# Moving S5 outputs and z tiles ahead of the last SSD units, and four weight loads at once

## The chip, the core and the metric

The kernel runs on one core of a Trainium2 chip. The metric is the device time of one launch in microseconds. A core has TensorE (PE in the profile), VectorE (DVE), ScalarE (ACT), GpSimd (POOL) and SyncE (SP), each with an instruction queue of its own that is worked off in order, and 16 DMA engines. Nearly all transfers of this kernel are issued by SP's queue: a transfer whose buffer isn't free holds back the transfers queued behind it.

## What is computed

A block of a bidirectional encoder on x of 2048 tokens by 1024 features, float32. Cut to what matters here:

```
h = rms_norm(x, norm_mix_w)
z, xbc, dt, u = split(h @ w_in)               # 1024 | 2048 | 32 | 512 columns
xbc = silu(dwconv5(xbc));  xs, B, C = split(xbc)
y1 = ssd_scan(forward) + ssd_scan(backward) + d * xs   # 16 heads, 4 groups, chunks of 128 tokens
y1 = rms_norm(y1 * silu(z), ssd_norm_w)
y  = s5_scan(u, forward) + s5_scan(u, backward) + d * u # 32 groups of 16 channels, 64 states
g  = gelu(y);  gl = g @ glu_w + glu_b          # per group, 16 -> 32
y2 = rms_norm(gl[:16] * sigmoid(gl[16:]), s5_norm_w)
x  = x + concat(y1, y2) @ w_out
up = dwconv3(rms_norm(x, norm_ffn_w) @ w_up);  val, gate = split(up)
x  = rms_norm(x + (silu(gate) * val) @ w_down, norm_final_w)
```

## The kernel before

Every float32 product is done as three matmuls of split operands: a high part hi and the rest lo, hi*hi (L444), lo*hi (L445) and hi*lo (L446). A weight or an activation is therefore split first, one cast on ScalarE and one operation on VectorE.

**Stages.** From 0 to 290 us the input is transposed (pt, L500), normalised and multiplied with u's columns of w_in (pu). Until 705 us the second half of the tokens is worked off, and beside it the S5 recursion, mainly on GpSimd. From 705 us the first half of the tokens: the four SSD groups, z tiles, and S5 outputs between them. From about 1187 us the out projection (the matmuls named p), then from 1560 us the FFN as Strassen products.

**A group** (L804) makes four conv tiles (each a projection of 128 columns over 1024 tokens, pmm, and its convolution on VectorE) and then eight SSD units, one for each chunk of 128 tokens. A **unit** (L742) loads decay rows (rw, L747), takes exponentials (L764), multiplies masks and scores (L766, L767), runs small matmuls (ptb L756 and L757, pyd L770 and L776, pst L791), puts together yy (L778, L779, L781), stores it to y_d (L783), and carries the state in sb (L790, L801, L802). A **z tile** (L698) projects 128 columns over 1024 tokens and stores them to z_d. **S5 outputs** (L369) of one index b are four groups of matmuls s5py (L386), Gelu to s5gt (L394), matmuls s5pgl (L400), a tanh (L403) and two operations to s5vl (L405, L406), stored to ys_d (L407).

**out_weights** (L813) splits w_out in twelve pieces (raw loads woraw into a pool of six buffers that the group's four conv tiles share; casts L824, splits L825). **out_pre** (L827) reads the results back: ztt from z_d (L832), yt from y_d (L834), ysT from ys_d (L867); yt times ztt (L851), a cast (L439), and the out matmuls.

**u_weights** (L535) loads u's columns of w_in in four pieces of 512 KB (L543) through two raw buffers (wraw) and splits each into wu.

**What sets the order.** Instructions are put on their engines by a scheduler that simulates a timeline, with the priority of the program's order. Tables at the head say where work is written: OC[g] holds the indices of the S5 outputs written ahead of group g (OC[4] behind group 3), ZC[g] the z tiles ahead of group g of the first half.

Of the kernel before, what the change touches and what calls it, by code (L numbers as in the profile page):

```python
# [21 lines left out]
S5W = 512  # L22
# [6 lines left out]
ZA = 4  # L29
GA = 4  # L30
ZB = ((4,), (5,), (6,), (7,))
OC = ((), (0, 1), (2, 3), (4, 5), (6, 7))
ZC = ((), (0,), (1, 2), (3,), (4, 5, 6, 7))


def bcast(ap, axis, n):
# [380 lines left out]
class Block:  # L417
# [114 lines left out]
            nc.scalar.activation(hi, pt, AF.Copy, scale=w)  # L532
            nc.vector.scalar_tensor_tensor(lo, pt, w, hi.bitcast(F32), ALU.mult, ALU.subtract)

    def u_weights(self, sp, wp):  # L535
        nc = self.nc
        wv = self.A["w_in"][0].rearrange("(k p) n -> p k n", p=P)
        self.wu = [sp.tile([P, 8, S5W], F32R, name=f"wu{j}") for j in range(2)]
        raw = lambda c: wp.tile([P, 8, P], F32, name="wraw", tag="wraw", bufs=2).rearrange("p k n -> p (k n)").rearrange(
            "p (k n) -> p k n", n=c)  # L540
        for k in range(0, 8, 2):
            r = raw(S5W)
            nc.sync.dma_start(r, wv[:, k:k + 2, W_U:W_U + S5W])  # L543
            self.split(self.wu[0][:, k:k + 2], self.wu[1][:, k:k + 2], r)
        self.wd = sp.tile([P, 8, 64], F32R, name="wd")
        r = raw(32)[:, 0:8]
        nc.sync.dma_start(r, wv[:, :, W_DT:W_DT + 32])
        self.split(self.wd[:, :, 0:32], self.wd[:, :, 32:64], r)
        self.us = [sp.tile([P, 2, 8, 64], F32, name=f"us{m}") for m in range(4)]
# [251 lines left out]
                v.tensor_tensor(S, S, bcast(self.decb[:, ch, 16 + 4 * g:16 + 4 * g + 4], 2, 64), ALU.mult)  # L801
                v.tensor_tensor(self.sb[:, g], self.sb[:, g], st[:, 256:512], ALU.add)  # L802

    def group(self, mp, wp, sp, ps, pp, ht, half, g):  # L804
        cols = [(8 + g, W_B + 128 * g), (12 + g, W_C + 128 * g),
                (2 * g, W_X + 256 * g), (2 * g + 1, W_X + 256 * g + 128)]
        sl = [self.conv_tile(mp, wp, ps, ht, half, mt, c0) for mt, c0 in cols]
        self.nc.sync.dma_start(self.ct_d[g][:, 1024 * half:1024 * half + 1024], sl[1])
        for c in range(7, -1, -1):
            self.ssd_unit(sp, pp, g, 8 * half + c, sl)  # L810
# [387 lines left out]
def hybrid_block_kernel(ctx: ExitStack, tc: tile.TileContext, *aps):  # L1198
    nc = tc.nc
    A = dict(zip(_INS, aps[:-1]))  # L1200
    b = Block(nc, tc, A, aps[-1])
# [6 lines left out]
    with ExitStack() as mix:  # L1208
# [14 lines left out]
        ht = b.new_ht(hp)  # L1223
# [3 lines left out]
        with pool(name="s0", bufs=1) as sp, right("s5cs") as cs:  # L1227
            with right("s5prm") as sr:
                b.norm_block(sp, wp, pp, ht, 0, 2)
                b.u_weights(sp, wp)  # L1230
                p0 = tc.cur_priority
                soon = lambda: tc.high_priority(offset=tc.cur_priority - p0)
                b.u_dt(sp, ps, ht, 0, 2)
                with soon():
                    b.norm_block(sp, wp, pp, ht, 1, 514)
                b.u_dt(sp, ps, ht, 1, 514)
                with soon():
                    for i in range(2):
                        nc.scalar.copy(ht[i][:, :, 0:2], ht[i][:, :, 1024:1026].bitcast(F32))
                for j in (2, 3):  # L1240
                    with soon():
                        b.norm_block(sp, wp, pp, ht, j, 512 * j - 1022)
                    b.u_dt(sp, ps, ht, j, 512 * j - 1022)
                with soon():
                    s5.params(cs, sr)
                    b.main_consts(mk, sr, s5.pst)
            with right("s5tab") as wk:
                with soon():
                    for k in range(NK5):
                        s5.tables(wk, k)  # L1250
                for m in range(ZA):
                    b.z_tile(wp, ps, ht, 1, m)
# [27 lines left out]
        with right("s5o") as so:  # L1280
            s5.out_setup(so)
            for g in range(4):
                for m in ZC[g]:
                    b.z_tile(wp, ps, ht, 0, m)
                for o in OC[g]:
                    s5.outputs(so, o)
                b.group(mp, wp, sp, ps, pp, ht, 0, g)
            for m in ZC[4]:
                b.z_tile(wp, ps, ht, 0, m)
            for o in OC[4]:  # L1290
                s5.outputs(so, o)
        lw.close()
        psg.close()
        wo = ExitStack()
# [2 lines left out]
        nc.vector.tensor_copy(decf, b.decb[:, :, 0:16])  # L1297
        b.decb = decf
        b.fst = wc.tile([P, 4, 256], F32, name="fst")
        b.nfw = b.col(mc, A["norm_ffn_w"][0], 8, "nfw")  # L1300
        b.out_weights(wc, mp)
        psb, psc = ExitStack(), ExitStack()
        ps = psb.enter_context(pool(name="psb", bufs=4, space=PSUM))
# [2 lines left out]
        pth = en(pool(name="pth", bufs=1, space=PSUM, side="right"))  # L1306
        pp = psc.enter_context(pool(name="ppb", bufs=1, space=PSUM, side="right"))
        gp = en(tc.tile_pool(name="gp", bufs=1, side="right", reuse_waits="tile"))
        with right("b1") as sp:
            pre = b.out_pre(sp, gp, ps, pp, 0)  # L1310
            h2 = None
            for ch in range(16):
                cur = pre
                if ch < 15:
                    pre = b.out_pre(sp, gp, ps, pp, ch + 1)
                else:
                    b.ffn_consts(mc, gp, ps)
                last, h2 = h2, b.out_gemm(sp, gp, ps, pp, ch, *cur)
                if ch:
                    b.out_tail(gp, pth, ch - 1, last)  # L1320
                if 10 <= ch < 14:
                    b.tok_sums(gp, 0, ch - 10)
# [48 lines left out]
```

## Time and profile before

| | us |
|---|---|
| median of three runs | 2923.3 |
| lowest and highest run | 2913.18, 2929.7 |
| the profiled execution, its time | 2930.28 |
| its span | 2928.5 |
| TensorE busy | 2701.5 (92%) |
| VectorE busy | 2197.4 (75%) |
| ScalarE busy | 1364.4 (47%) |
| GpSimd busy | 653.9 (22%) |
| mean granted TensorE clock | 0.968 |

The rows are read as follows. A busy share over the whole span mixes stages, so the windows by stage come first. In a timeline each line is one instruction, or a few alike, with its start, its duration, and in brackets how long the engine had stood idle before it and what it then waited for. Durations of instructions that follow each other closely overlap a little. A clock of 1.00 is 2.4 GHz, 0.50 is 1.2 GHz.

### The profile page before, as it was taken

To read this page: it belongs to the slowest core of one execution; us is meant where nothing else is said; L and a number is where in the kernel's file an instruction comes from. 1 tells how busy PE (TensorE), PEld (TensorE's weight loads), DVE (VectorE), ACT (ScalarE), POOL (GpSimd) and SP (SyncE) were. 2 spreads that over 40 slices of the span, in tenths; PEclk is the share of its full clock that TensorE was granted. 3 is DMA by queue.
4 is the path that set the end of the run, shared out by engine and by line. 5 is a ranking of instruction groups with operands and counts; after the bars stand their busy time and mean duration, and the time that the engine had idled before them with its cause. 6 is when DMAs were issued, how large, how long until landed. Compare 5 with 4: busy or idle time off the path is not lost.

```text
span 2928.5 us, 37294 instructions
## 1 busy us (share of the span) xinstructions
PE 2701.5 (92%) x12952; PEld 2181.7 (74%) x12952; DVE 2197.4 (75%) x3255; ACT 1364.4 (47%) x2329; POOL 653.9 (22%) x1133
## 2 busy tenths in 40 slices
PE   6998899876999998899898999999999999999997
PEld 4666899765877886677776878787877777877776
DVE  5997688786786776677767777779887888656587
ACT  4542455444567665334235444446444445333254
POOL 0443499992233332111120000000000000000012
PEclk9999999988999999999998999999999999999999
DMA  4546633448455656957845234325444337456464
GB/s 129 173 133 198 168 114 121 112 128 227 134 175 162 188 163 204 252 170 201 252 141 187 79 108 137 107 77 193 149 136 130 121 131 243 160 204 194 150 233 158
DMA packets 507400, 471.55 MB, mean 161 GB/s; under 512 B 90364, under 2 KB 417356, under 8 KB 507212
## 3 DMA queue, kind: packets, MB, share of 16 engines
q1 hardware_dynamic: 504972, 463.99, 52.4%
q0 software_dynamic: 2240, 5.18, 0.7%
q8 instruction: 102, 1.67, 0.2%
q14 instruction: 86, 0.70, 0.1%
HBM read 324.37 MB, written 144.67 MB: 160 GB/s over the span
## 4 chain that ended last, share of the span: by engine, by line
PE 40%; DMA 8%; DVE 7%; issue 2%; ACT 2%; POOL 1%; SPq 0%; ACTq 0%; DVEq 0%; POOLq 0%
PE pA L1040 17%; PE pB L1040 9%; PE pD L1040 5%; PE p L444 3%; PE p L445 2%; PE p L446 2%; DMA ar<-act_d 2%; DVE ll L440 1%; DMA bs<-in_ffn_w_down_dram 1%; DMA wr<-in_ffn_w_up_dram 1%; DMA bs<-hop_d 1%; DMA wt_d<-bs 1%; PE po L846 1%; DVE tl L1027 1%; DMA tst<-in_ffn_w_down_dram 0%
## 5 line engine op out<-in xcount | busy, mean ns | idle before, releaser
L1040 PE MATMUL pA<-th,lh 128*128 128x512 f32 x1056 | 423.7, 402 | 28.3 <-ACT pc L1088 18.8
L1040 PE MATMUL pA<-tl,lh 128*128 128x512 f32 x1056 | 422.1, 400 | 4.2 <-DVE tl L1027 4.2
L1040 PE MATMUL pA<-th,ll 128*128 128x512 f32 x1056 | 420.5, 399 | 0.8 <-DVE ll L440 0.8
L444 PE MATMUL pmm<-hh,wh 128*128 128x512 f32 (+1 forms) x896 | 333.9, 373 | 3.7 <-DVE zt L706 2.4
L445 PE MATMUL pmm<-hl,wh 128*128 128x512 f32 (+1 forms) x896 | 332.7, 371 | 0.0
L446 PE MATMUL pmm<-hh,wl 128*128 128x512 f32 (+1 forms) x896 | 330.2, 369 | 0.0
L1040 PEld LDWEIGHTS pA<-th,lh 128*128 128x128 f32 x1056 | 200.6, 190 | 86.7 <-ACT pc L1088 27.4
L1040 PEld LDWEIGHTS pA<-tl,lh 128*128 128x128 f32 x1056 | 200.7, 190 | 54.2 <-DVE tl L1027 6.4
L1040 PEld LDWEIGHTS pA<-th,ll 128*128 128x128 f32 x1056 | 200.6, 190 | 50.3 <-DVE ll L440 1.6
L1040 PE MATMUL pB<-tl,lh 128*128 128x512 f32 x528 | 209.6, 397 | 1.8 <-DVE tl L1027 1.8
L1040 PE MATMUL pB<-th,lh 128*128 128x512 f32 x528 | 209.7, 397 | 1.8 <-ACT lh L439 1.6
L1040 PE MATMUL pB<-th,ll 128*128 128x512 f32 x528 | 209.2, 397 | 0.0
L1088 ACT COPY pc<-pA 128x512 f32<-128x512 f32 x204 | 116.0, 584 | 185.4 <-PE pA L1040 184.4
L444 PEld LDWEIGHTS pmm<-hh,wh 128*128 128x128 f32 x896 | 169.9, 190 | 30.2 <-issue 3.7
L445 PEld LDWEIGHTS pmm<-hl,wh 128*128 128x128 f32 x896 | 169.8, 190 | 22.6 <-issue 2.5
L764 ACT ACTIVATE Lt<-rw,tokS 128x128 f32<-128x128 f32 x512 | 157.4, 389 | 61.3 <-PE pyd L770 48.7
L446 PEld LDWEIGHTS pmm<-hh,wl 128*128 128x128 f32 x896 | 169.6, 189 | 21.3 <-issue 1.1
L692 DVE SCALAR_TENSOR_TENSOR xbc<-rb,cw,xbc 128x1024 f32<-128x1024 f32 x128 | 178.7, 1399 | 3.8 <-ACT xbc L690 2.8
L444 PE MATMUL p<-wo,yh 128*128 128x512 f32 x384 | 157.3, 410 | 22.2 <-ACT yh L439 21.3
L439 ACT CAST lh<-s 128x512 fp32r<-128x512 f32 (+3 forms) x136 | 109.1, 815 | 123.8 <-DVE s L1007 71.2
L440 DVE TENSOR_TENSOR ll<-s,lh 128x1024 fp32r<-128x1024 f32 (+3 forms) x136 | 126.3, 933 | 52.5 <-PE pA L1040 43.7
L445 PE MATMUL p<-wo,yh 128*128 128x512 f32 x384 | 155.6, 405 | 0.0
(421 smaller groups left out, 6139.0 us busy)
## 6 DMA issues: line engine op xcount, KB each, us to landing
wr<-in_ffn_w_up_dram SPq DMA_DIRECT2D x88, 512.0 KB
rw<-acs_d SPq DMA_DIRECT2D x128, 256.0 KB
wraw<-in_w_in_dram SPq DMA_DIRECT2D x52, 512.0 KB
ar<-act_d SPq DMA_DIRECT2D x32, 512.0 KB
yp_d<-cv SPq DMA_DIRECT2D x32, 512.0 KB
cv<-yp_d SPq DMA_DIRECT2D x32, 512.0 KB
tst<-hop_d SPq DMA_DIRECT2D x28, 512.0 KB
act_d<-cv SPq DMA_DIRECT2D x22, 512.5 KB
```

The lines of the kernel that those rows point to most:

```text
L439: self.nc.scalar.copy(hi, src)
L440: self.nc.vector.tensor_tensor(lo, src, hi.bitcast(F32), ALU.subtract)
L444: mm(ps, lhs[0], rhs[0], start=first, stop=False)
L445: mm(ps, lhs[0], rhs[1], start=False, stop=False)
L446: mm(ps, lhs[1], rhs[0], start=False, stop=last)
L692: nc.vector.scalar_tensor_tensor(ac, rb[:, j:j + 1024], cw(j), ac, ALU.mult, ALU.add)
L764: nc.scalar.activation(Lt[:, d, h], rw[:, d, h], AF.Exp, bias=tk(0, d, h))
L846: nc.tensor.matmul(po[:, 2 * (g - 2 * q) + j], self.fst[:, g, 128 * j:128 * j + 128], ct[:, g], start=True, stop=True)
L1027: nc.vector.tensor_tensor(l, st[:, 0:n], h.bitcast(F32), ALU.subtract)
L1040: mm(ps, x, y, start=first and k == i == 0, stop=k == kt - 1 and i == 2, skip_group_check=not first)
L1088: self.nc.scalar.copy(t, src)
```

## The change

Three edits, all of order and place:

- S5 outputs: three ahead of group 1, three ahead of group 2, two ahead of group 3, none behind it. The last four z tiles are no longer written behind group 3 but between its conv tiles and its units.
- u_weights: the third and fourth raw pieces go into two buffers that S5's tables use later (kt, named rb in the rows), so that no load waits for a buffer.
- The column of norm_ffn_w (nfw, 128x8 elements of 4 bytes) lives in another pool, opened with the out stage.

```
-OC = ((), (0, 1), (2, 3), (4, 5), (6, 7))
-ZC = ((), (0,), (1, 2), (3,), (4, 5, 6, 7))
+OC = ((), (0, 1, 2), (3, 4, 5), (6, 7))
+ZC = ((), (0,), (1, 2), (3,))
...
-            r = raw(S5W)
+            r = raw(S5W) if k < 4 else kt[k // 2 - 2].rearrange("p h g o -> p (h g o)").rearrange("p (k n) -> p k n", n=S5W)
...
-    def group(self, mp, wp, sp, ps, pp, ht, half, g):
+    def group(self, mp, wp, sp, ps, pp, ht, half, g, between=lambda: None):
...
         sl = [self.conv_tile(mp, wp, ps, ht, half, mt, c0) for mt, c0 in cols]
+        between()
...
-                b.u_weights(sp, wp)
+                b.u_weights(sp, wp, s5.kt)
...
                 for o in OC[g]:
                     s5.outputs(so, o)
-                b.group(mp, wp, sp, ps, pp, ht, 0, g)
-            for m in ZC[4]:
-                b.z_tile(wp, ps, ht, 0, m)
-            for o in OC[4]:
-                s5.outputs(so, o)
+                rest = lambda: [b.z_tile(wp, ps, ht, 0, m) for m in range(4, 8)]
+                b.group(mp, wp, sp, ps, pp, ht, 0, g, rest if g == 3 else lambda: None)
...
-        b.nfw = b.col(mc, A["norm_ffn_w"][0], 8, "nfw")
         b.out_weights(wc, mp)
...
+        b.nfw = b.col(gp, A["norm_ffn_w"][0], 8, "nfw")
```

TensorE, from the last z matmul (pmm) on, in the kernel before (s5py and s5pgl are S5 outputs, the others belong to SSD units):

```order
L446 MATMUL pmm<-hh,wl 128x512
L386 MATMUL s5py<-s5uTo,s5tz 128x128
L386 MATMUL s5py<-s5st,s5ot 128x127
L776 MATMUL pyd<-xbc,sb 128x128 x2
L791 MATMUL pst<-xw,xb 128x256
L756 MATMUL ptb<-ident,xbc 128x128 x3
L757 MATMUL ptb<-xbc 128x128
L386 MATMUL s5py<-s5st,s5ot 128x127
L791 MATMUL pst<-xw,xb 128x256
L770 MATMUL pyd<-Lt,xb 64x128 x4
L400 MATMUL s5pgl<-s5gt,s5bd 128x256 x2
```

The same place in the changed kernel:

```order
L446 MATMUL pmm<-hh,wl 128x512
L791 MATMUL pst<-xw,xb 128x256
L757 MATMUL ptb<-xbc 128x128
L756 MATMUL ptb<-ident,xbc 128x128 x3
L757 MATMUL ptb<-xbc 128x128
L791 MATMUL pst<-xw,xb 128x256
L770 MATMUL pyd<-Lt,xb 64x128 x4
L756 MATMUL ptb<-ident,xbc 128x128 x3
L757 MATMUL ptb<-xbc 128x128
L776 MATMUL pyd<-xbc,sb 128x128 x2
L791 MATMUL pst<-xw,xb 128x256
```

Behind the last z matmul stood five units mixed with eight S5 groups; now seven units stand there and nothing else until the out matmuls.

VectorE in the same stretch, before (L825 splits w_out, L405 and L406 are S5's):

```order
L778 TENSOR_TENSOR yy<-eb,pyd 128x256
L801 TENSOR_TENSOR sb<-sb,decb 128x256
L406 SCALAR_TENSOR_TENSOR s5vl<-s5tht,s5vl 128x256
L779 TENSOR_TENSOR yy<-yy,pyd 128x256
L825 SCALAR_TENSOR_TENSOR wo_10989<-woraw,onw,wo_10988 128x1024
L781 SCALAR_TENSOR_TENSOR yy<-xbc,dsk,yy 128x128 x2
L825 SCALAR_TENSOR_TENSOR wo_10989<-woraw,onw,wo_10988 128x1024
L405 TENSOR_SCALAR s5vl<-s5pgl,s5gb 128x256
L802 TENSOR_TENSOR sb<-sb,pst 128x256
```

And in the changed kernel (L826 is the split of w_out):

```order
L802 TENSOR_TENSOR sb<-sb,pst 128x256
L826 SCALAR_TENSOR_TENSOR wo_10985<-woraw,onw,wo_10984 128x1024
L767 TENSOR_TENSOR Lt<-Lt,ptb 128x512
L790 TENSOR_TENSOR xw<-xb,tokS 128x256 x2
L778 TENSOR_TENSOR yy<-eb,pyd 128x256
L801 TENSOR_TENSOR sb<-sb,decb 128x256
L766 TENSOR_TENSOR Lt<-Lt 128x512
L779 TENSOR_TENSOR yy<-yy,pyd 128x256
L826 SCALAR_TENSOR_TENSOR wo_10985<-woraw,onw,wo_10984 128x1024
L781 SCALAR_TENSOR_TENSOR yy<-xbc,dsk,yy 128x128 x2
L802 TENSOR_TENSOR sb<-sb,pst 128x256
```

All twelve splits now stand between the operations of units, and no S5 operation is left there.

SP's queue in the first microseconds, the piece from S5's columns (L228) on (dsk is ssd_d, s5craw the C matrices, wraw raw weights):

```order
 L716 DMA mcr<-in_ssd_conv_w_dram 80x128
+L547 DMA wraw<-in_w_in_dram 128x8x32
 L717 DMA mcr<-in_ssd_conv_b_dram 16x128
-L725 DMA dsk<-in_ssd_d_dram 64x8x1
-L543 DMA wraw<-in_w_in_dram 128x2x512
-L725 DMA dsk<-in_ssd_d_dram 64x8x1
-L424 DMA nfw<-in_norm_ffn_w_dram 128x8x1
-L543 DMA wraw<-in_w_in_dram 128x2x512
+L725 DMA dsk<-in_ssd_d_dram 64x8x1 x2
+L660 DMA wraw<-in_w_in_dram 128x8x128
 L219 DMA s5craw<-in_s_c_re_bwd_dram 128x4x64
 L219 DMA s5craw<-in_s_c_im_bwd_dram 128x4x64
```

The two later pieces of u's weights have left this place for the head of the queue, right behind the first two, and nfw has left it for the out stage, where it stands ahead of the first ztt and yt. The two loads of ssd_d still stand ahead of the backward C matrices.

## Rows read from the trace of the kernel before

**Rows 1.** Windows by stage: window and length, then busy PE, PEld, DVE, ACT, POOL; clock; DMA; GB/s

```profile
705.00:1128.00 423.00, 415.86 (x2234) 341.59 (x2232) 317.27 (x504) 255.47 (x505) 122.15 (x114) 1.00 0.59 164
1128.00:1187.50 59.50, 37.62 (x217) 30.71 (x215) 38.16 (x68) 34.81 (x60) 8.95 (x14) 0.84 0.82 245
1187.50:1560.00 372.50, 335.41 (x1617) 273.80 (x1617) 255.40 (x413) 130.93 (x247) 68.75 (x211) 0.95 0.72 203
1560.00:2928.50 1368.50, 1318.49 (x5547) 1046.87 (x5547) 1032.95 (x1310) 617.14 (x800) 36.10 (x141) 0.99 0.46 152
```

**Rows 2.** Windows of 10 us in the tail

```profile
1150.00:1160.00 10.00, 5.95 (x22) 3.67 (x22) 6.94 (x16) 2.25 (x4) 0.99 (x2) 0.67 0.91 248
1160.00:1170.00 10.00, 9.44 (x52) 8.30 (x51) 5.68 (x9) 5.67 (x8) 1.13 (x3) 0.76 0.99 335
```

**Rows 3.** TensorE by line, 1128 to 1187.5: busy us, mean ns | idle before, releaser

```profile
L386 PE MATMUL s5py<-s5st,s5ot 128*128 128x127 f32 x60 | 10.3, 296 | 0.4 <-DMA s5ot<-s5od 0.4
L386 PE MATMUL s5py<-s5uTo,s5tz 128*128 128x128 f32 (+1 forms) x44 | 9.9, 336 | 3.6 <-DMA s5uTo<-u_d 3.6
L400 PE MATMUL s5pgl<-s5gt,s5bd 128*128 128x256 f32 x32 | 9.6, 427 | 8.3 <-ACT s5gt L394 8.3
...
L446 PE MATMUL pmm<-hh,wl 128*128 128x512 f32 x1 | 0.4, 392 | 0.0
```

**Rows 4.** Timeline of TensorE at the tail's edges: start, duration, instruction, [idle before]

```profile
1127.69 0.39 PE L446 MATMUL pmm<-hh,wl 128*128 128x512 f32 x1
...
1187.52 0.79 PE L444 MATMUL p<-wo,yh 128*128 128x512 f32 x1 [9.17 <-ACT yh L439]
```

**Rows 5.** VectorE by line, 1128 to 1187.5

```profile
L825 DVE SCALAR_TENSOR_TENSOR wo<-woraw,onw,wo 128x1024 fp32r<-128x1024 f32 x12 | 15.5, 1294 | 8.8 <-ACT wo L824 8.8
...
L781 DVE SCALAR_TENSOR_TENSOR yy<-xbc,dsk,yy 128x128 f32<-128x128 f32 x10 | 3.3, 374 | 0.0
L790 DVE TENSOR_TENSOR xw<-xb,tokS 128x256 f32<-128x256 f32 x5 | 3.0, 636 | 0.0
...
L778 DVE TENSOR_TENSOR yy<-eb,pyd 128x256 f32<-128x256 f32 x5 | 2.1, 413 | 0.0
L767 DVE TENSOR_TENSOR Lt<-Lt,ptb 128x512 f32<-128x512 f32 x3 | 2.0, 683 | 0.5 <-ACT xb L759 0.5
```

**Rows 6.** Timeline of VectorE, two units of the tail

```profile
1155.45 0.41 DVE L778 TENSOR_TENSOR yy<-eb,pyd 128x256 f32<-128x256 f32 x1
1155.78 0.42 DVE L801 TENSOR_TENSOR sb<-sb,decb 128x256 f32<-128x256 f32 x1
...
1165.34 0.41 DVE L778 TENSOR_TENSOR yy<-eb,pyd 128x256 f32<-128x256 f32 x1
```

**Rows 7.** Timeline of ScalarE: two casts of w_out in the tail

```profile
1161.68 2.43 ACT L824 ACTIVATE wo<-woraw,onw 128x1024 fp32r<-128x1024 f32 x2 [6.60 <-DMA woraw<-in_w_out_dram]
```

**Rows 8.** Timeline of SP's queue at the end of the tail

```profile
1168.69 0.92 SPq L783 DMA_DIRECT2D y_d<-yy  x1
...
1174.45 4.17 SPq L407 DMA_DIRECT2D ys_d<-s5vl  x2
...
1179.25 0.53 SPq L834 DMA_DIRECT2D yt<-y_d  x1
```

**Rows 9.** Timeline of TensorE at the start

```profile
22.88 0.39 PE L444 MATMUL pu<-hh,wu 128*128 128x512 f32 x1
32.36 1.06 PE L222 MATMUL s5pc<-ident,s5craw 128*64 128x128 f32 x4 [9.09 <-DMA s5craw<-in_s_c_re_bwd_dram]
...
44.09 0.60 PE L500 MATMUL pt<-ident,xt 128*128 128x128 f32 x4
```

**Rows 10.** DMA between 18 and 27.5 us

```profile
DMA packets 1169, 0.53 MB, mean 56 GB/s; under 512 B 913, under 2 KB 913, under 8 KB 1169
```

**Rows 11.** Timeline of SP's queue at the start: the column of norm_ffn_w

```profile
19.03 2.56 SPq L424 DMA_DIRECT2D nfw<-in_norm_ffn_w_dram  x1
```

More of the change, by code (lines that the diff above doesn't have):

```diff
@@ L533, in norm_again, with u_weights @@
             nc.vector.scalar_tensor_tensor(lo, pt, w, hi.bitcast(F32), ALU.mult, ALU.subtract)
-    def u_weights(self, sp, wp):
+    def u_weights(self, sp, wp, kt):
         nc = self.nc
```

## The prediction

> **What bounds the kernel now.** I read the views from coarse to fine. The busy time by stage comes first: from 705 to 1128 us TensorE is busy 415.9 of 423 us at clock 1.00, from 1128 to 1187.5 only 37.6 of 59.5 at clock 0.84, and the out stage behind it is again near full [rows 1]. So nothing that merely reorders filled stages can gain. What can gain is the hole between the last tile of z and the first matmul of the out projection, which I call the tail. Cut into slices of 10 us, one slice has TensorE busy 5.95 at clock 0.67, the next 9.44 at 0.76 with the DMA queues at 0.99 [rows 2]. The grouped matmuls say what is run there: the two S5 output lines L386 and L400, with the waits on s5gt (8.3 us) and on one load of s5uTo (3.6) [rows 3]. The timeline gives the edges: the last z matmul at 1127.69, and the first matmul of the out stage, L444, at 1187.52, after 9.17 us in which TensorE had nothing [rows 4]. The second place is the start: TensorE stands 9.09 us until 32.36, by the profile for the load of the backward C matrices [rows 9].
>
> The profiled execution took 2930.28 us (span 2928.5), 7.0 above the median of the three runs. I work out differences against the profiled one and add them to the median.
>
> **The tail, part by part.** The change computes S5 outputs 6 and 7 ahead of group 3 and puts the last four z tiles between that group's conv tiles and its units. No arithmetic is added or dropped in this stage.
>
> What leaves the hole: the eight S5 groups of L386 and L400. Their three rows are 29.8 us of the 46.1 that the nine rows of that view sum to (first and last shown; the records overlap) [rows 3]. That share of the 37.6 busy us is 24.3, and at the stage's clock of 0.84 it is 20.4 us of work at full clock [rows 1, 3]. It now lies in a stage where TensorE is full, so it is paid there: the last z matmul comes some 20 us later. Against it, more units fall behind the last z: seven now, five before. The rest of the busy time, 13.3 us at 0.84, is 11.2 us for five units, 2.2 a unit, so two units take 4.4 us out of the full stage. The last z matmul moves from 1128 to 1128 + 20.4 - 4.4 = 1144.
>
> What is left in the hole: seven units in a row and the twelve splits of w_out (L825, L826 in the changed kernel), with no other matmuls between them. TensorE needs 7 x 2.2 = 15 us for that and doesn't bound it. VectorE does. By the changed order it has, between its last z eviction and the out stage, 12 operations of the price of L767 (0.683), 13 of L790 (0.636), 27 of L778 and its like (0.413), 14 of L781 (0.374), and 12 of L825 (1.294) [rows 5]: 8.2 + 8.3 + 11.2 + 5.2 = 32.9 for the units, 15.5 for the splits, 48.4 in all. Back to back they start closer together than their durations: L801 starts 0.33 us behind an L778 of 0.41 [rows 6]. At that ratio of 0.8 the units cost 26.5 and the sum is 42. I take 43, nearer to the lower end because the trace shows it for consecutive operations. The last yy is then at 1144 + 43 = 1187, where the kernel before has its last y_d store issued at 1168.69 [rows 8].
>
> The splits can't run ahead. Two buffers are free for the raw weights while the group lives, and a round trip was long: ScalarE stood 6.60 us for woraw at 1161.68 [rows 7]. A pair costs about that wait, one 1.1 us cast and one 1.3 us split, near 9 us; the ten loads behind the first two need 5 x 9 = 45. That is the same size as VectorE's 43, so I add nothing, and keep the excess for the range.
>
> What the end gains: in the kernel before, the store of the last y_d was issued at 1168.69, but SP stood 4.17 us with S5's own stores at 1174.45 and issued the load of yt only at 1179.25 [rows 8]; 8.27 us later the first out matmul ran [rows 4, 8]. With the S5 stores gone that detour goes: behind the last yy I put 2.2 us for the store and the three loads ahead of yt in SP's queue, and the same 8.3 us: 10.5. The column of norm_ffn_w, now in that queue, is inside the 2.2 if it is issued like its neighbours (0.5) and 2 us more if it takes its 2.56 of before [rows 11]; I keep that for the range. The out stage then begins at 1187 + 10.5 = 1197.5, 10 us later than before. The out stage and the FFN behind it are full on TensorE and move as a whole [rows 1]. **Tail: +10 us**, from -1 (VectorE's 26.5 for the units and four splits of 1.3 only, the others done earlier) to +18 (48.4 and 2 us of the weight loop on top).
>
> On the clock: the slice with little TensorE work had 0.67, the dense stage 1.00 [rows 1, 2]. The seven units alone will run at 0.5 to 0.7. At 0.5 their 15 us become 30, still under VectorE's 43, so I charge nothing. The Trainium skill ("TensorE: Matmul & The Clock Gate", Part 1) says that the throttled state is the default and that activity releases it, which speaks against taking the S5 matmuls out from between the units; the slices here agree with its direction.
>
> **The start.** Four loads of u's weights are issued at once instead of two and two, so the casts and splits of the second half come early. Before, six blocks of transposes and matmuls follow the gap, from 32.36 to 44.69: 2.06 us each [rows 9]. By the changed order two of the six stand ahead of the matmul that waits for the backward C matrices: -4.1. That load still waits behind the two columns of ssd_d, whose single-element packets make up most of the 1169 packets that moved in the 9.5 us from 18 to 27.5 with 0.53 MB [rows 10]; the norm_ffn_w column (2.56 us of issue) is no longer in that queue: -2 [rows 11]. The extra 1 MB of bulk goes ahead of everything: at the 335 GB/s of the best slice [rows 2] it delays the rows behind it by 3.1. **Start: -3 us**, from -9 (the whole gap closes) to +3 (the bulk delays and nothing moves ahead).
>
> The Trainium skill ("DMA: Bandwidth & Descriptors", section Bandwidth, Measured) gives a floor of about 10.5 ns a packet, by which the 1024 packets of ssd_d would take, as an estimate, under 1 us on 16 engines and the gap would close fully. The measured window has 1169 packets in 9.5 us, so the measurement decides; by the page's figure the start would be -9 and the total 2924.
>
> **Sum:** -3 + 10 = +7: the profiled execution would be 2937, the median 2930.
>
> **The rivals.**
> *S5 was the bound of the tail* (faster). For it: the waits on s5gt and s5uTo are 11.9 us of the hole [rows 3], and 4.17 us of SP's queue go [rows 8]. If five of the twelve splits are done before the last z eviction, VectorE has 43 - 5 x 1.29 = 36.5 left, the out stage begins at 1191, +3; if all the woraw loads are early too and the units run at VectorE's 26.5 plus four splits, 1144 + 31.7 + 10.5 = 1186.2, -1. With the whole 9 us at the start that is -10: 2913. Against it: two buffers for the weights.
>
> *Units at the weight loop's pace* (slower). Where the loop's wait stood in front of a unit, from 1155.45 to 1165.34, a unit took 9.9 us [rows 6]. ScalarE's casts stand in its queue ahead of the units' exponentials, and VectorE's splits behind these casts. Seven units at 9.9 are 69 us, the out stage begins at 1144 + 69 + 10.5 = 1223.5, +36; with the start, 2956. It is slower by over 0.5% (14.6 us, about what a measurement of this kernel can tell from no change) from a tail of +17.6 on, a unit every 7.2 us. For it: that is what the one stretch without filler shows. Against it: S5's loads no longer share the queues, which stood at 0.99 [rows 2].
>
> *Nothing moves.* The S5 work costs as much in the full stage as it gave the hole and the unit chain shortens by the same, the start's gap only moves: 0, so 2923.
>
> **How the numbers follow.** Forecast 0.45, with its own range from 2918 (tail +1, start -6) to 2941 (tail +18, start 0); faster rival 0.17; slower rival 0.23; nothing moves 0.15. Over 0.5% faster is below 2908.7: half of the faster rival, 0.09. Over 0.5% slower is above 2937.9: nearly the whole slower rival (0.20) and the upper end of the forecast (0.07), 0.27. The rest, 0.64, lies within. The range 2914 to 2948 leaves out the far half of each rival.
>
> **What will show it.** Right: the last z matmul near 1144 minus the start's gain; then seven units 6 us apart, VectorE busy over 80%, clock under 0.8; first L444 near 1195; at the start a matmul gap that still ends with the backward C load, at 32 to 34 us. Wrong: units under 5 us apart (the faster rival) or over 7 (the slower); a gap of less than 3 us at the start; an out stage whose own length changes by more than 5 us, for which this sum has no term.

## The result

The changed kernel takes 2961.64 us (2954.77 to 2962.83, four runs) where the kernel before takes 2925.41 (2913.18 to 2929.7): the ratio is 1.0126, interval 1.0091 to 1.0161. It is slower by 36 us. The prediction was 2930 us, with a range up to 2948. The profiled executions are 2962.83 and 2930.28 us, 32.6 apart, and are compared below.

First the windows of the changed kernel, with its own edges: the first S5 output matmul (757.9; the matmul itself starts at 758.1, in the kernel before at 751.3), the last z matmul (1154.6), the first out matmul (1219.2) and the first matmul of the FFN (1594.0). The fourth window is the stretch of the units in the tail. The columns are window and length, busy PE, PEld, DVE, ACT, POOL, clock, DMA share, GB/s.

```profile
757.90:1154.60 396.70, 384.08 (x2080) 317.87 (x2079) 270.79 (x431) 233.57 (x446) 107.09 (x110) 0.99 0.58 160
1154.60:1219.20 64.60, 29.30 (x148) 19.86 (x147) 45.40 (x80) 31.90 (x70) 8.41 (x6) 0.67 0.66 188
1219.20:1594.00 374.80, 337.43 (x1616) 275.35 (x1616) 253.18 (x410) 128.50 (x245) 66.06 (x211) 0.95 0.71 199
1155.60:1205.20 49.60, 28.30 (x143) 18.95 (x141) 44.17 (x79) 30.19 (x68) 8.41 (x6) 0.71 0.64 196
```

The same edges of the kernel before, which answer to [rows 1]:

```profile
751.10:1127.70 376.60, 369.46 (x2010) 304.30 (x2009) 279.05 (x443) 232.64 (x457) 108.88 (x102) 1.00 0.57 162
1127.70:1187.50 59.80, 37.92 (x218) 30.97 (x216) 38.16 (x68) 34.81 (x60) 8.95 (x14) 0.84 0.82 243
1187.50:1557.80 370.30, 334.65 (x1616) 273.54 (x1617) 253.20 (x410) 128.84 (x245) 68.75 (x211) 0.96 0.72 202
```

| stretch | before, us | after, us | difference | predicted |
|---|---|---|---|---|
| to the first S5 output matmul | 751.1 | 757.9 | +6.8 | -3 |
| to the last z matmul (the full stage) | 376.6 | 396.7 | +20.1 | +16 |
| to the first out matmul (the tail) | 59.8 | 64.6 | +4.8 | -6 |
| out stage | 370.3 | 374.8 | +4.5 | 0 |
| the rest | 1370.7 | 1367.0 | -3.7 | 0 |

The full stage and the tail together hold 24.9 of the 32.5 us. TensorE's busy time in them rose by 6.0 us (384.08 + 29.30 against 369.46 + 37.92, at the lower clock of the tail), its idle time by 18.9: 5.5 in the full stage, 13.4 in the tail. The S5 work that had filled the tail was taken out, but the tail did not get shorter (+4.8), and the full stage grew by 14.6 us of matmuls and 5.5 of waits.

The edges and the pace of the tail in the changed kernel. TensorE's timeline, to be read against [rows 4] and [rows 9]:

```profile
35.10 1.03 PE L222 MATMUL s5pc<-ident,s5craw 128*64 128x128 f32 x4 [8.91 <-DMA s5craw<-in_s_c_re_bwd_dram]
...
1154.58 0.40 PE L446 MATMUL pmm<-hh,wl 128*128 128x512 f32 x1
...
1219.22 0.76 PE L444 MATMUL p<-wo,yh 128*128 128x512 f32 x1 [14.77 <-ACT yh L439]
```

VectorE's, to be read against [rows 6] (a unit is timed here by the start of its L778; the last yy ends at 1205.16):

```profile
1164.45 0.42 DVE L778 TENSOR_TENSOR yy<-eb,pyd 128x256 f32<-128x256 f32 x1
...
1176.30 0.41 DVE L778 TENSOR_TENSOR yy<-eb,pyd 128x256 f32<-128x256 f32 x1
...
1184.44 0.41 DVE L778 TENSOR_TENSOR yy<-eb,pyd 128x256 f32<-128x256 f32 x1
...
1203.63 0.42 DVE L778 TENSOR_TENSOR yy<-eb,pyd 128x256 f32<-128x256 f32 x1 [0.79 <-PE pyd L776]
```

The seven units, so timed, stand between 1159.17 and 1203.63, 7.4 us apart on average, up to 11.9. ScalarE's casts of the raw weights stand between them and wait for the loads, six times, 10.6 us in all ([rows 7] has 6.60 in one). Here are the longest wait and a late one, and what waited in turn: VectorE's split, with the unit of 1176.30 behind it in the queue, and TensorE's pst, for ScalarE's copy of the state (sf), which stands behind the cast:

```profile
1170.58 1.15 ACT L825 ACTIVATE wo<-woraw,onw 128x1024 fp32r<-128x1024 f32 x1 [5.04 <-DMA woraw<-in_w_out_dram]
1171.77 1.28 DVE L826 SCALAR_TENSOR_TENSOR wo<-woraw,onw,wo 128x1024 fp32r<-128x1024 f32 x1 [3.51 <-ACT wo L825]
...
1197.25 1.15 ACT L825 ACTIVATE wo<-woraw,onw 128x1024 fp32r<-128x1024 f32 x1 [1.82 <-DMA woraw<-in_w_out_dram]
1198.31 0.35 ACT L795 COPY sf<-pst 128x256 f32<-128x256 f32 x1
1198.71 0.70 PE L791 MATMUL pst<-xw,xb 128*128 128x256 f32 x2 [1.43 <-ACT sf L795]
```

SP's queue, to be read against [rows 8]. The two z stores hold the queue for 12.38 us, and the decay rows of a unit are issued behind them, at 1141.50. At the end the load of fst waits 2.8 us for the store of the last state (1204.93), and yt is issued 5.0 us behind the last yy:

```profile
1122.16 12.38 SPq L707 DMA_DIRECT2D z_d<-zt  x2
1141.50 0.80 SPq L747 DMA_DIRECT2D rw<-acs_d  x2
...
1204.93 0.32 SPq L796 DMA_DIRECT2D sf_d<-sf  x1
1205.34 0.38 SPq L783 DMA_DIRECT2D y_d<-yy  x1
1208.65 0.32 SPq L855 DMA_DIRECT2D fst<-sf_d  x1
1209.06 0.39 SPq L424 DMA_DIRECT2D nfw<-in_norm_ffn_w_dram  x1
1209.54 0.53 SPq L833 DMA_DIRECT2D ztt<-z_d  x1
1210.16 1.69 SPq L835 DMA_DIRECT2D yt<-y_d  x1
```

### The profile page after: what moved, and what is told of

The parts are those of the page before. It is cut to its first block, busy times and chain, and to the rows that moved or that the text cites. A ratio compares the mean times of both kernels' runs of the same rounds, so it can differ in the third digit from the quotient of the medians.

```text
span 2961.0 us, 37290 instructions
## 1 busy us (share of the span) xinstructions
PE 2706.2 (91%) x12952; PEld 2188.4 (74%) x12952; DVE 2196.3 (74%) x3255; ACT 1362.3 (46%) x2328; POOL 652.5 (22%) x1133
## 4 chain that ended last, share of the span: by engine, by line
PE 58%; DMA 16%; DVE 15%; issue 4%; ACT 4%; SPq 2%; POOL 1%; DVEq 0%; ACTq 0%; POOLq 0%
PE pA L1041 16%; PE pB L1041 9%; PE pD L1041 5%; PE pmm L444 4%; PE pmm L445 4%; PE pmm L446 4%; PE p L444 3%; PE p L445 3%; PE p L446 2%; DMA ar<-act_d 2%; DMA rw<-acs_d 2%; PE s5py L386 2%; DVE ll L440 1%; DVE xbc L692 1%; DMA s5xi<-s5xd 1%
## 5 line engine op out<-in xcount | busy, mean ns | idle before, releaser
L1041 PEld LDWEIGHTS pA<-th,ll 128*128 128x128 f32 x1056 | 200.7, 190 | 50.6 <-DVE ll L440 3.9
```

The costliest lines, as they stand in the source:

```text
L1041: mm(ps, x, y, start=first and k == i == 0, stop=k == kt - 1 and i == 2, skip_group_check=not first)
```

## The experiments

All but the last column come from a profiled execution of each kernel: the full stage (first S5 output matmul to last z matmul), the tail (from there to the first out matmul) and their sum, in us. The ratio is of the times, to the kernel before as measured beside it, with its interval.

| kernel | full stage | tail | sum | ratio |
|---|---|---|---|---|
| before | 376.6 | 59.8 | 436.4 | 1 |
| the change | 396.7 | 64.6 | 461.3 | 1.0126 (1.0091 to 1.0161) |
| e1 loads only | 376.7 | 58.9 | 435.6 | 1.0012 (0.9994 to 1.0031) |
| e2 nfw only | 377.8 | 60.7 | 438.5 | 1.0024 (1.0004 to 1.0044) |
| e3 order only | 398.2 | 61.1 | 459.3 | 1.0104 (1.0074 to 1.0134) |
| e4 S5 only | 409.4 | 41.3 | 450.7 | 1.0056 (1.0029 to 1.0083) |
| e5 z only | 372.8 | 72.7 | 445.5 | 1.0056 (1.0038 to 1.0074) |
| e6 change, no VectorE splits | 397.4 | 62.2 | 459.6 | 1.0105 (1.0080 to 1.0129) |
| e7 change, two weights | 398.7 | 47.5 | 446.2 | 1.0039 (1.0019 to 1.0059) |
| e8 one S5 output behind | 397.2 | 48.2 | 445.4 | 1.0053 (1.0032 to 1.0074) |
| e9 before, two weights | 382.7 | 56.2 | 438.9 | 0.9988 (0.9971 to 1.0004) |
| e10 change, seven buffers | 406.4 | 63.5 | 469.9 | 1.0137 (1.0117 to 1.0157) |
| e11 before, three buffers | 376.9 | 57.7 | 434.6 | 1.0001 (0.9982 to 1.0020) |
| e12 S5 only, seven buffers | 409.5 | 41.3 | 450.8 | 1.0058 (1.0034 to 1.0082) |
| e13 nfw, padded | 374.6 | 62.0 | 436.6 | 1.0061 (1.0043 to 1.0080) |
| e14 change, padded | 397.5 | 63.5 | 461.0 | 1.0121 (1.0087 to 1.0155) |
| e15 three S5 outputs behind | 361.8 | 81.9 | 443.7 | 1.0059 (1.0040 to 1.0079) |
| e16 five z tiles behind | 383.2 | 56.5 | 439.7 | 1.0042 (1.0028 to 1.0056) |
| e17 change, seven buffers, no splits | 406.0 | 57.0 | 463.0 | 1.0121 (1.0073 to 1.0169) |
| e18 change, loads without work | 402.2 | 52.1 | 454.3 | 1.0061 (1.0039 to 1.0083) |

The kernels with the order of before (before, e1, e2, e11, e13) have sums of 434.6 to 438.5, those with the order of the change (the change, e3, e14) 459.3 to 461.3: the sum repeats within 4 us, and the more than 20 us between the two groups are clear of that. The sum doesn't hold all of a ratio: by the ratios most kernels lose more than by their sums, the change 12 us more, e8 7, e15 10, e16 9, and e13 18 us where its sum has none. That part lies ahead of the first S5 output or behind the first out matmul, or in what a single profiled execution differs by from the others; no run tells which.

### Which edit costs

e1 is the second edit alone, e2 the third, e3 the first:

```
e1 to e4 differ from before by one edit of the change or a part of it; one line of each is shown, the others are left out
e1: +            r = raw(S5W) if k < 4 else kt[k // 2 - 2]...
e2: +        b.nfw = b.col(gp, A["norm_ffn_w"][0], 8, "nfw")
e3: +OC = ((), (0, 1, 2), (3, 4, 5), (6, 7), ())   and between() in group
e4: +OC = ((), (0, 1, 2), (3, 4, 5), (6, 7), ())   z tiles 4 to 7 behind group 3 as before
```

> The kernel before with the four loads of u's weights at once, and nothing else of the change. In the changed kernel the wait for the backward C matrices ended 2.7 us later (35.10 against 32.36) and the first conv operation of the second half 2.5 us later. Theory A (the cost of the change lies in the order of S5 outputs, z tiles and units): +2 to +5 us here, all of it there by the first conv operation. Theory B (the earlier loads turn the scheduler's order over, and the second half and the dense stage lose by that): +12 to +20 us, most of it behind 345 us. The prediction on record would have -3 (its start term).

> The kernel before with the column of norm_ffn_w loaded ahead of the out stage, and nothing else of the change. Theory A: -2 to +2 us; the start gains about 2 us at the backward C matrices (gap ends at 30 to 31 instead of 32.36), the load of yt in front of the out stage loses at most 2. Theory C (its 1024 packets of 4 bytes hold back ztt, yt and ysT and lengthen the out stage, 4.5 us longer in the changed kernel): +4 to +7 us, between the last yy and the end of the out stage.

> The kernel before with both edits of order (S5 outputs 3, 3, 2 ahead of groups 1 to 3, the last four z tiles between the conv tiles and the units of group 3), without the edits of the start. Theory A: +24 to +32 us: the last z matmul 18 to 22 us later, the stretch from there to the first out matmul 3 to 8 us longer, as in the changed kernel (+27 of which 7 was there before, and +4.8). Theory B: +10 to +18 us.

> The kernel before with the S5 outputs moved (3, 3, 2 ahead of groups 1 to 3) and the last four z tiles still written behind group 3. It tells the two edits of order apart. If the S5 outputs alone cost (20 us of matmuls moved from a stage with holes into a full one, and units left alone at the end): +15 to +30 us, the tail no shorter than 55 us. If the z tiles between are the harm (their stores hold SP's queue, 12.4 us at 1122 in the changed kernel, in front of the units' decay rows): -10 to +8 us, with z tiles left as filler between the units and under five units behind the last z matmul.

The order is the cost: e3 carries 1.04 of the change's 1.26%, and its sum is that of the change within 2 us. Theory A had its time (+24 to +32 us) and its last z matmul (20.2 us later) right, but not its tail: 61.1 is 1.3 us longer, not 3 to 8. Theory B falls: the loads alone measure within 0.3% of nothing. The loss by the first conv operation that theory A expected of them isn't there either (342.3 against 342.7). e2 is 0.24% slower, which is above theory A's 2 us, and not where theory C had it: from the last yy to the end of the out stage it takes 389.3 us, the kernel before 389.6. Its first S5 output is late, at 760.9, against 751.3.

The windows of e3 (full stage, tail), nearly those of the change:

```profile
749.70:1147.90 398.20, 384.68 (x2079) 318.49 (x2077) 268.25 (x430) 233.34 (x446) 108.12 (x110) 0.99 0.57 159
1147.90:1209.00 61.10, 29.77 (x149) 20.59 (x147) 45.29 (x81) 32.01 (x70) 8.53 (x6) 0.67 0.72 199
```

e4 fell outside its first case (its tail is 41.3, not over 55) and above its second: the S5 move alone costs 14.3 us of sum, 32.8 in the full stage for 18.5 gained behind it.

### The two edits of order, and their reverse

```
e5:  OC of before;  between() with z tiles 4 to 7 in group 3
e8:  -OC = ((), (0, 1), (2, 3), (4, 5), (6, 7))   +OC = ((), (0, 1), (2, 3, 4), (5, 6), (7,))
e15: -OC = ((), (0, 1), (2, 3), (4, 5), (6, 7))   +OC = ((), (0, 1), (2, 3), (4,), (5, 6, 7))
e16: -ZC = ((), (0,), (1, 2), (3,), (4, 5, 6, 7)) +ZC = ((), (0,), (1, 2), (), (3, 4, 5, 6, 7))
```

> The kernel before with only the last four z tiles moved between the conv tiles and the units of group 3; S5 outputs 6 and 7 stay behind it. With the S5 move alone at +0.56% and both edits of order at +1.04%, the theory that the two costs add gives +8 to +20 us here: no z matmul is left as filler among the last units, but the S5 groups are. The theory that the harm of the z move needs the S5 groups gone (units alone at the end) gives -3 to +5 us.

> The kernel before with S5 outputs 2, 3, 2 ahead of groups 1 to 3 and one, not two or none, behind group 3; z tiles as before. If each S5 output taken out of the tail costs alike: half of the +0.56% of moving both, +5 to +10 us. If the tail has more S5 work than it can hide, and less than none is too little: 0 to -10 us, the tail shorter by more than the 10 us that the dense stage then grows.

> The kernel before with the S5 outputs moved the other way: three instead of two behind group 3, one ahead of it. One behind cost 9 us between the first S5 output and the first out matmul, none 14. If S5 work is cover for the tail as long as the weight loop runs, and two just fill it: 0 to +8 us here, the tail longer by more than the dense stage shortens. If the trend goes on: -5 to -10 us, and this is the better version.

> The kernel before with z tile 3 also written behind group 3, so that five z tiles, not four, are filler among its last units. Writing the z tiles ahead of the units cost 9 us. If more filler helps: -3 to -8 us, the last z matmul later, the tail shorter by more. If the tail is held by the S5 groups and the weight loop anyway: within 3 us.

The z move alone costs 9.1 us of sum, the S5 move 14.3, both 22.9: they add, as the first case of e5 had it. By the number of S5 outputs behind group 3 the sum is 450.7 (none), 445.4 (one), 436.4 (two), 443.7 (three), and by the ratios none, one and three are each half a per cent slower than two. So of these four the two outputs of the kernel before fill its tail best, and this is not a trend that a better version could follow: e15 shortens the full stage by 15 us and lengthens the tail by 22. By their sums e8 (+9.0) and e15 (+7.3) lie in their first cases, by their ratios (+16 and +17 us) above them. With five z tiles behind (e16) the sum is 3.3 us up, about what it varies by, and the kernel 0.42% slower; the hoped gain isn't there.

The windows of e4 and e15 show the exchange:

```profile
748.00:1157.40 409.40, 396.39 (x2154) 327.74 (x2153) 284.72 (x460) 243.68 (x478) 112.47 (x114) 0.98 0.58 161
1157.40:1198.70 41.30, 13.64 (x74) 8.50 (x72) 30.87 (x52) 22.75 (x39) 2.60 (x2) 0.65 0.82 237
```

```profile
749.60:1111.40 361.80, 356.94 (x1932) 292.84 (x1931) 273.72 (x426) 218.63 (x435) 101.58 (x94) 1.00 0.56 157
1111.40:1193.30 81.90, 50.65 (x295) 42.16 (x293) 47.03 (x85) 40.81 (x76) 15.72 (x22) 0.82 0.74 226
```

Without any S5 work behind it (e4) the tail has 13.6 us of matmuls in 41.3, so TensorE doesn't make it last. The last yy ends there at 1182.1, the last cast of w_out at 1191.3, and yt is issued at 1192.6, right behind: the weights end last.

### What holds the units of the tail

```
e6:  VectorE's split (lo) made for k < 2 only; the out projection uses lo of k % 2
e7, e9: for k in range(2): load, cast, split; the out projection uses hi and lo of k % 2
e10, e12: the raw pieces in a pool opened behind S5's, bufs=7, not "xbc" of the group
e11: every third raw piece in one buffer of its own
e17: e10 with e6
e18: pieces 2 to 11 loaded through the two buffers, one column of each copied by GpSimd
```

> The changed kernel without ten of the twelve VectorE splits of w_out (the low parts of pieces 2 to 11 aren't made; the out projection uses those of pieces 0 and 1 in their place), all loads and casts kept. From the last z matmul to the last yy the changed kernel took 50 us with VectorE busy about nine tenths of it. If VectorE's sum sets the units' pace: 10 x 1.2 = 12 us less there, 2950 us in all. If the round trip of the weight loads does, through ScalarE's casts in front of the units' exponentials: 0 to -4 us. If the units' own chain does: 0 to -4 us as well, and the next kernel tells these two apart.

> The changed kernel with two of the twelve pieces of w_out loaded, cast and split (the out projection uses these two in place of all): no weight loop in the tail. If VectorE sets the pace: -12 to -16 us against the changed kernel, hardly more than without the splits alone. If the weight loop's loads and casts set it: -15 to -25 us, while the kernel without the splits alone gains under 4. If the units' chain does: under -5 us in both.

> The kernel before with two of the twelve pieces of w_out loaded, cast and split (the out projection uses these two in place of all). In the changed kernel this cut took 17 us out of the stretch from the last z matmul to the first out matmul. If the weight loop holds the tail of the kernel before as well: -10 to -20 us there. If the eight S5 groups do, and hide the loop: 0 to -6 us. In the second case the change turned a hidden loop into the bound.

> The changed kernel with the raw pieces of w_out in seven buffers of their own, in the space that S5's output tiles leave, instead of two; all work is done. If the round trip of the two buffers set the pace: -10 to -17 us against the changed kernel, ratio to the kernel before 1.005 to 1.009, the tail 48 to 55 us instead of 64.6. If the loads' traffic or the work of casts and splits set it: 0 to -5 us.

The stretch of the seven units in e6 and, above, in the changed kernel (1155.60 to 1205.20):

```profile
1152.40:1201.60 49.20, 29.65 (x142) 19.44 (x140) 30.16 (x69) 29.82 (x67) 7.84 (x6) 0.67 0.63 198
```

VectorE falls from 44.17 us (89% of the stretch) to 30.16 (61%), and the stretch from 49.6 to 49.2. So VectorE, busy as it was, didn't set the pace. Its busy time is also not all work: some 4 us of the 44.17 are four operations that took over three times as long as the same operations elsewhere in the stretch (two L790 2.82 us for 0.76, two L781 2.62 for 0.61), while GpSimd ran the masks of the decay rows (L753, at 1173.41 and 1178.51). In the whole changed kernel the 18 L781 that overlap such a mask take 1.35 us in the median, the 110 others 0.35.

```profile
1173.57 2.82 DVE L790 TENSOR_TENSOR xw<-xb,tokS 128x256 f32<-128x256 f32 x2
1179.10 2.62 DVE L781 SCALAR_TENSOR_TENSOR yy<-xbc,dsk,yy 128x128 f32<-128x128 f32 x2
```

Without the loads, casts and splits of ten pieces the tail does get shorter: 47.5 us in e7, 17.1 less than in the change, as its second case had it. The clock rose with it, from 0.67 to 0.84, and the same 148 matmuls are busy 23.5 us for 29.3; so up to 5.8 of the 17.1 us can be the clock's, which no run varied by itself. The kernel before loses only 3.6 us of tail by the same cut (e9), and by the ratio nothing that can be measured: the loop was mostly covered there.

```profile
1158.20:1205.70 47.50, 23.53 (x148) 16.60 (x147) 33.70 (x71) 21.50 (x60) 8.79 (x6) 0.84 0.57 147
```

e10 missed. Seven buffers take nearly all waits for the loads away from ScalarE, but the tail stays at 63.5 and the full stage grows to 406.4. Its ScalarE timeline shows what came in place: the casts stand together, seven of them between two units' exponentials, and behind a wait for the norm's column, onw. That load was issued late, from 1173.73 on, behind three z stores that held SP's queue for 26.17 us.

```profile
1178.89 4.27 ACT L825 ACTIVATE wo<-woraw,onw 128x1024 fp32r<-128x1024 f32 x4 [4.06 <-DMA onw<-in_ssd_norm_w_dram]
1183.06 0.46 ACT L759 COPY xb<-ptb 128x384 f32<-128x384 f32 x1
1183.42 3.23 ACT L825 ACTIVATE wo<-woraw,onw 128x1024 fp32r<-128x1024 f32 x3
1186.55 2.44 ACT L764 ACTIVATE Lt<-rw,tokS 128x128 f32<-128x128 f32 x8
```

> The kernel before with a third buffer for the raw pieces of w_out (one of their own in the space left beside S5's output tiles). If the weight loop holds its tail: -3 to -8 us. If the S5 groups do: within 2 us.

> The S5 outputs moved, the z tiles behind group 3 as in the kernel before, and the raw pieces of w_out in seven buffers in the space that S5's output tiles leave. Without the buffers this order was 14 us slower from the first S5 output to the first out matmul (409.4 + 41.3 against 376.6 + 59.8 us). If two buffers were the reason: the last 41 us become 28 to 32, the whole 0 to +4 us against the kernel before; this is the version that could beat it. If not: +10 to +15 us.

> The changed kernel with the raw pieces of w_out in seven buffers and without ten of the twelve VectorE splits (their low parts aren't made; those of pieces 0 and 1 are used in their place). Alone, neither edit shortened the 64.6 us from the last z matmul to the first out matmul by more than 2.4. If two limits of like size stand there, the round trip of two buffers and VectorE's sum, both gone gives 48 to 55 us, as with two pieces (47.5). If the loads' traffic or ScalarE's casts are the limit: 60 to 65 us.

> The changed kernel with all twelve raw pieces of w_out loaded through the two buffers, but ten of them neither cast nor split (GpSimd copies one column of each, so that the buffer has a reader; the out projection uses pieces 0 and 1 in place of all). If the casts in ScalarE's queue, with their wait for the loads, hold the units' exponentials: 47 to 52 us from the last z matmul to the first out matmul, as with two pieces. If the loads' traffic in the queues does: 58 to 65 us.

e11 is the kernel before in time, full stage and tail: a third buffer is worth nothing there. e12 has e4's two numbers again (409.5 and 41.3), by another way: the last cast of w_out ends 24 us behind the last z matmul, not 34, and the last yy 30, not 25. So the buffers by themselves don't make that order shorter, and no version here that does all the work beats the kernel before.

e18 keeps the loads and drops the work on them: 52.1 us, at the edge of its first case. Of the 17.1 us that the ten pieces cost, 12.5 go with casts and splits, and 4.6 (52.1 - 47.5) stay, with the loads or with the clock, which is 0.70 here. The splits alone are 2.4 (e6). e18 differs from e6 by ten casts less (and ten small GpSimd copies more), and its tail is 10.1 us shorter, at a clock of 0.70 for 0.64: most of the cost goes with the casts, which wait in ScalarE's queue for the loads. What they hold up there is less the exponentials, which run ahead (those of the last unit end at 1190.9, its yy at 1205.2), than the short copies of a unit. In the changed kernel TensorE's pst waits 7.9 us in all for sf, and where the splits are gone (e6) VectorE's L767 waits 12.1 us for xb. With the change's order and all work the tail varies from 61.1 (e3) to 64.6 between profiled executions. So the 2.4 of e6 and the 1.1 of e10 can't be told from nothing, and the 17.1, 12.5 and 10.1 are known within some 4 us.

Waits behind the last z matmul (in all, times, longest), of the changed kernel, then of e6:

```profile
PE pst L791 <- ACT sf L795: 7.9, 4, 3.4
DVE Lt L767 <- ACT xb L759: 12.1, 3, 4.9
```

e18's tail, and a line of its ScalarE:

```profile
1155.00:1207.10 52.10, 28.44 (x149) 19.54 (x147) 32.16 (x71) 21.61 (x60) 11.19 (x16) 0.70 0.82 234
1182.73 1.28 ACT L764 ACTIVATE Lt<-rw,tokS 128x128 f32<-128x128 f32 x4 [2.74 <-POOL rw L753]
```

Without the casts the exponentials wait for the masked decay rows (rw), which lie in two buffers too, 5.6 us in four waits. Whether this is the next limit isn't shown: no run varied these two buffers.

e17 came out between its two cases: 57.0. Both the buffers and the splits gone give 7.6 us of tail, more than the 1.1 and 2.4 of each alone, and less than the 12.5 of the work as a whole; the twelve casts of about 1.1 us are still in that queue. Its full stage is as long as e10's, and its ratio no better than the change's.

### The start

> The kernel before with the norm_ffn_w column loaded ahead of the out stage, and a dummy tile of the same 32 bytes a partition left in its old pool, so that every tile behind it lies where it lay in the kernel before. In the five kernels with the column moved, the DMA queues were busy 0.53 to 0.55 of 60 to 120 us, in the nine without 0.43 to 0.45, for the same GB/s, and the first conv operation came at 344.9 to 348.2 instead of 340.5 to 343.5. If the addresses are the reason: share back at 0.43 to 0.45, first conv operation at 340 to 344, ratio to the kernel before 0.998 to 1.001. If the load's place in the queue is: share 0.53 to 0.55 and 345 to 348 as without the dummy, ratio 1.002 to 1.003.

> The changed kernel with the same dummy tile. If the addresses cost it 3 to 5 us: ratio to the kernel before 1.009 to 1.011 instead of 1.0126, share 0.43 to 0.45 in 60 to 120 us, first conv operation 340 to 344. If not: 1.012 to 1.014.

```
e13, e14: +        pad = mc.tile([P, 8], F32, name="pad")   in the place where nfw lay
```

Windows of 60 to 120 us of before, e2 and e13, in this order:

```profile
60.00:120.00 60.00, 55.45 (x267) 37.85 (x266) 56.65 (x117) 28.81 (x62) 26.57 (x26) 0.94 0.43 123
```

```profile
60.00:120.00 60.00, 55.15 (x269) 37.75 (x268) 56.59 (x112) 29.33 (x62) 29.01 (x26) 0.97 0.53 127
```

```profile
60.00:120.00 60.00, 55.81 (x269) 37.86 (x268) 56.61 (x112) 29.20 (x62) 26.34 (x26) 0.94 0.44 127
```

The dummy of 32 bytes brings the DMA share back from 0.53 to 0.44 (0.55 to 0.46 in e14): the addresses behind it set how long the queues are busy for the same rate. But the time did not follow. e13 is 0.61% slower than before, not equal to it, and e14 is 1.0121, inside the changed kernel's interval, with its first conv operation at 351.8. So the addresses explain the share and not the cost: e13 lies above both of its cases, and what makes it slower stays open. The theory that the addresses cost the change 3 to 5 us falls.

## Why the prediction was wrong

**The step that failed** is the one on the weight loop: "That is the same size as VectorE's 43, so I add nothing, and keep the excess for the range." It took two limits of equal size as one, and VectorE as the one. The runs showed VectorE's sum as the lesser: it may be cut from 89 to 61% busy with hardly an effect on the units' pace (e6). Loading, casting and splitting ten pieces of w_out costs the tail 17.1 us (e7), most of it with the casts in ScalarE's queue (e18 against e6), which the sum had not added up. From the last z matmul to the end of the last yy the changed kernel took 50.6 us (1154.6 to 1205.2), where 43 stood in the sum: +7.6.

That is not the whole miss. The profiled difference was 32.5 us where +7 stood, and the 25.5 us too much are 10.8 in the tail, 4.1 in the full stage, 9.8 ahead of it, 4.5 in the out stage and -3.7 behind. The two edits of order alone are enough to leave the range: 1.0104 (e3) on 2925 us is 2956, and the range ended at 2948.

**The slower rival was the right one in kind.** It named this queue ("ScalarE's casts stand in its queue ahead of the units' exponentials") and its line of decision, a unit every 7.2 us; the units came 7.4 us apart. What the casts held up was a unit's copies (sf, xb) and the splits rather than the exponentials. Its price of 9.9 us was too high for all seven; that its 2956 us lies only 6 under the measured median is luck, by errors that cancelled. It was held back by "S5's loads no longer share the queues", which was true (DMA share 0.66 after 0.82); the units were no faster for it.

**The last z matmul** was put at 1144 less 3 for the start, and came at 1154.6. The full stage grew by 20.1, the working had 20.4 - 4.4 = 16. TensorE's busy time in it grew by 14.6, near the working; the rest is waits, for which it had no term. TensorE waited 7.4 us for s5uTo in the changed kernel's full stage, against 1.9 in that of before (in all, times, longest; before, then after):

```profile
PE s5py L386 <- DMA s5uTo<-u_d: 1.9, 1, 1.9
PE s5py L386 <- DMA s5uTo<-u_d: 7.4, 3, 3.7
```

The other 9.8 come from ahead of it (+6.8 where -3 stood).

**The start.** The gap that the prediction expected to end at 32 to 34 us ended at 35.10, still behind the backward C matrices, 8.91 us long. The bulk's delay was right (2.7 for 3.1). The gain ahead of the gap was one block of transposes and matmuls, not two: 16 transposes and 14 matmuls of u's columns stand ahead of it, 12 and 8 in the kernel before. Even so the four loads gained later: in the eight kernels with them the last matmul of u's columns starts at 196.3 to 197.8 us, in the twelve others at 200.1 to 203.2. The step that failed is that all behind the start would move with it: the first conv operation comes at 345.2 in the changed kernel and 342.3 in e1, against 342.7 before. What holds it wasn't followed.

That ssd_d's single-element packets hold the gap is borne out by the changed kernel's trace, though no run took them out. From 22 to 30 us the DMA engines moved nothing but 859 packets of 4 bytes, 9.3 ns for each, and the load of the C matrices stood 6.65 us in SP's queue meanwhile:

```profile
DMA packets 859, 0.00 MB, mean 0 GB/s; under 512 B 859, under 2 KB 859, under 8 KB 859
22.40 6.65 SPq L219 DMA_DIRECT2D s5craw<-in_s_c_re_bwd_dram  x1
```

The Trainium skill ("DMA: Bandwidth & Descriptors", section Bandwidth, Measured) gives about 10.5 ns a packet, from 0.67 us for a transfer of 64 packets, issued there from GpSimd. The prediction divided this once more, by 16 engines; undivided it makes, as an estimate, 10.8 us for 1024 packets. The trace, at 9.3 ns, agrees with that. So the page's figure did not speak for a gap that closes.

**The end of the tail.** From the last yy to the first out matmul 10.5 us were predicted, 14.1 measured (1205.2 to 1219.2). The 2.2 for stores and loads ahead of yt were 5.0: the load of fst stands first in SP's queue and waited 2.8 us for the last state's store, and the column of norm_ffn_w takes 0.5. The rest is the 9.1 from the issue of yt to the matmul, for 8.3. In e3 the last state was stored 2.5 us ahead of the last y_d, fst didn't wait, the column isn't there, and yt was issued 2.2 us behind the last yy, as predicted; the whole stretch is 11.0 (1198.0 to 1209.0).

**Right:** the S5 work's price in the full stage in size, the unit count behind the last z matmul, the clock (0.67 in the tail and 0.71 in the units' stretch, forecast 0.5 to 0.7), that VectorE would be over 80% busy, though not what was made of it, and that TensorE's own work would not bound the units.

**Open.** Where the 6.8 us ahead of the first S5 output come from. In nine kernels with the norm_ffn_w column moved that matmul is at 752.2 to 764.6, mean 758; in the eleven others, before among them, at 745.5 to 756.6, mean 751. The means differ, but the ranges overlap: nine of the eleven run everything in the same order on all engines until past 840 us and still lie 11 us apart, so one profiled execution doesn't tell 6.8 us from that. The dummy tile ruled out only the addresses. The out stage's 4.5 longer and the FFN's 3.7 shorter weren't followed either. That the z stores in SP's queue keep units from running beside the z tiles is read from the timeline and wasn't tried by itself.

## What to carry to other kernels

Work that stands among waits costs less than the same work in a full stage, but it isn't free: taking two S5 outputs out of the tail gave back 18.5 us there and cost 32.8 in the full stage (e4). Before moving filler out of a stretch, ask what else lasts there, and take that stretch without the filler as the new bound. Two limits of the same size on different engines don't simply hide behind each other when their instructions stand in one dependent chain; add up every in-order queue on it, ScalarE's too, with what stands ahead of the chain's next step. And the reverse edits, one step each way, tell cheaply whether an order sits at its best.

## What was not expected of the hardware

The share of time in which the DMA queues are busy depends on where the tiles lie: with all tiles behind one pool moved by 32 bytes a partition, it rose from 0.43 to 0.53 at 123 and 127 GB/s in the same stretch, and fell back to 0.44 with a dummy tile in the gap. No loss of time was tied to it here. Dropping 14 us of VectorE's busy time out of a stretch where it was 89% busy shortened that stretch by 0.4 us. VectorE's L781, 0.35 us alone, took 1.35 beside GpSimd's masks. And from 22 to 30 us of the changed kernel nothing moved but packets of 4 bytes, one every 9.3 ns, with the DMA engines otherwise idle.
